# First scale of a decoder step by quarters, x first in the load queue, and inverse roots on turned columns

## The chip, the cores and the metric

The kernel runs on one core of one Trainium2 chip. The metric is the device time of one launch in microseconds. A core has five engines that run side by side and wait for each other through semaphores: TensorE (PE in the profile; PEld is its weight load) multiplies into PSUM, VectorE (DVE) and ScalarE (ACT) do elementwise work, GpSimd (POOL) does elementwise work on SBUF and issues some loads, and SyncE (SP) issues nearly all loads. The transfers themselves run on 16 DMA engines.

## The reference

One inference step of a one-layer recurrent decoder, in float32, for a prompt of 256 tokens and 8 sample sequences of 4 tokens, so for 288 token columns, with a model width of 2048. Nine condition vectors (one for the prompt, eight for the samples) give the adaLN shift, scale and gate. Cut to what matters here:

```python
mod = silu(c) @ w_ada + b_ada                      # c is (9, 2048), w_ada is (2048, 6*2048)
sh1, sc1, gt1, sh2, sc2, gt2 = split(mod, 6)
xn = rmsnorm(x, g_norm1) * (1.0 + sc1) + sh1       # rmsnorm: x * rsqrt(mean(x*x) + eps) * g
proj = xn @ w_in                                   # parts for a linear recurrence, GLA, mLSTM and gates
...                                                # three branches, each with its own norm and output product
x = x + gt1 * (merged @ w_out)
xn = rmsnorm(x, g_norm2) * (1.0 + sc2) + sh2
x = x + gt2 * (square(relu(xn @ w_ff1)) @ w_ff2)
y = rmsnorm(x, g_final)
```

The outputs are y and the new states of the three branches.

## The kernel before

Activations lie with features on the 128 partitions: x is 16 tiles (k = 0 to 15) of 128 features by 288 columns, eight tiles in each of the two slots xa and xb. Ten such slots of SBUF (s0 to s9) are used in turn for everything.

**Projections.** `stream` computes one block of 512 output features. A group is two k tiles of weights, 512 KB: `raw` is loaded on SP, ACT rounds it to `hi` (L156), DVE takes the rest `lo` = raw - hi (L157), and PE multiplies hi by the rounded activation xh, hi by its rest xl, and lo by xh (L163 to L165), so 4 x 2 x 3 = 24 matmuls of 288 columns a group. There are three buffers of each of raw, hi and lo. At the end of a block `evac` copies or adds the four PSUM banks to a slot: `to_slot` on ACT (L452), `plus_slot` on DVE (L463).

**Products with the conditions.** `cond_product` yields load units. A unit is a load of `w_ada` of 1 MB on SP into a slot, the ring tile or a pair of `st` tiles (the list `slots["ids"]` says which, in turn), and products of the nine conditions with it (L256): the output columns are dealt to four groups of 32 PE columns, so matmuls come in groups of four that run at once. After the last unit of a product `end` turns the result back with transposes of 32 by 32 blocks (L219), and `ada_finish` adds the bias (L278) and, for a scale, multiplies with g (L281). `units` lists all units in order: the scale of the first norm (SC1) in two halves of eight units each (`sc0`, `sc`), the shift (SH1) in 16, then a correction of the early projections for the shift (`cor`), and the rest.

**Order.** SP runs in the order of the program. On the other engines a planner orders the instructions by priority and by its own estimate of when they are ready, and each engine then runs its list in order. `every` gives a pattern with one word for each group of a stream: L loads the next unit, V (`visit`) multiplies all loaded units, right behind the last matmul so far; `drain` loads and multiplies until a product is done.

**The first stage.** x is loaded on ACT's queue while SP loads the eight units of `sc0`. ACT squares the 16 tiles, a product with ones sums them (L442), and `rstd_of` gives the inverse root as exp(-0.5 ln(..)) (L386, L387), each function with its own table load on ACT. Then `scale1(0)` makes xn without its shift for k = 0 to 7: `modulate` multiplies x by the root into a second tile (L395), scales the prompt columns on DVE (L400) and the sample columns on GpSimd (L402), and `split` makes xh (L424) and xl (L425). Three early blocks (NPRE, the features of q, k and half of v) run over k = 0 to 7, then, when `sc` is done, over k = 8 to 15 and are added. Meanwhile the units of the shift are multiplied, with the pattern

```python
every("L LV " * 4 + "L LLV L LV " * 3 + "LV" + " ." * 40)
```

`whole` rebuilds the scaled activation from xh and xl on GpSimd (L407), `shift` adds the shift (L414, L416) and splits again, and all further blocks use the result. The early blocks lack the shift's part, which `cor` adds later.

**Other inverse roots.** `rstd_of` serves the second norm (near 1172 us) and the final norm as well. `rows_rsqrt` serves the norms of the two branches (near 550 and 840 us): Sqrt on ACT over 288 columns and a reciprocal of 288 columns on DVE (L648). In `ev_o` a small activation with Ln (L1217) loads that table ahead of the second norm.

Of the kernel before, what the change touches and what calls it, by code (L numbers as in the profile page):

```python
# [14 lines left out]
P = 128  # L15
# [37 lines left out]
def trunk(ctx, tc, io):  # L53
# [149 lines left out]


    ct, th9 = (t288()[:, 0:KT * 9].rearrange("p (k c) -> p k c", k=KT) for _ in range(2))
# [35 lines left out]
    def cond_product(name, load, each, cols, stat, finish):  # L241
# [4 lines left out]
        def products(raw, q):  # L246
            if not acc_:
                acc_.append(pa.tile([P, 512], F32, tag="pa", name=nm("pa")))
# [26 lines left out]
    def ada_finish(kind):  # L275
        def finish(h, pv):
            o = mod[:, kind, 8 * h:8 * h + 8, :]
            V.tensor_tensor(out=o, in0=pv[:, :, 0:9], in1=bada[:, kind, 8 * h:8 * h + 8].unsqueeze(2).to_broadcast([P, 8, 9]), op=ALU.add)  # L278
            if kind in (SC1, SC2):
                gg = Pm("g1" if kind == SC1 else "g2")  # L280
                V.scalar_tensor_tensor(o, o, 1.0, gg[:, 8 * h:8 * h + 8].unsqueeze(2).to_broadcast([P, 8, 9]), ALU.add, ALU.mult)  # L281
        return finish
# [6 lines left out]
    def ada(kind):  # L289
# [92 lines left out]

    def rstd_of(ps):
        r = row("lf")
        with tc.high_priority():
            S.activation(r, ps[:, :N], AF.Ln, bias=eps, scale=1.0 / D)  # L386
            S.activation(r, r, AF.Exp, scale=-0.5)  # L387
        return r
# [4 lines left out]
    def modulate(xg, rs, k0, fk, xh, xl, xr):  # L393

        V.tensor_tensor(out=xr, in0=xg, in1=rs.unsqueeze(1).to_broadcast([P, 4, N]), op=ALU.mult)  # L395
        bc = [P, 2, NB, TS]
        for j in range(0, 4, 2):
            r = slice(k0 + j, k0 + j + 2)
            for i in range(j, j + 2):
                V.tensor_scalar(xr[:, i, 0:NP], xr[:, i, 0:NP], mod[:, fk, k0 + i, 0:1], None, ALU.mult)  # L400
            xs = smp(xr[:, j:j + 2])
            G.tensor_tensor(out=xs, in0=xs, in1=mod[:, fk, r, 1:9].unsqueeze(3).to_broadcast(bc), op=ALU.mult)  # L402
            split(xh[:, r, :], xl[:, r, :], xr[:, j:j + 2])

    def whole(k0, xh, xl, xr):

        G.tensor_tensor(out=xr, in0=xh[:, k0:k0 + 4, :].bitcast(F32), in1=xl[:, k0:k0 + 4, :].bitcast(F32), op=ALU.add)  # L407

    def shift(k0, shk, xh, xl, xr):

        for j in range(0, 4, 2):
            r = slice(k0 + j, k0 + j + 2)
            for i in range(j, j + 2):
                V.tensor_scalar(xr[:, i, 0:NP], xr[:, i, 0:NP], mod[:, shk, k0 + i, 0:1], None, ALU.add)  # L414
            xs = smp(xr[:, j:j + 2])
            V.tensor_tensor(out=xs, in0=xs, in1=mod[:, shk, r, 1:9].unsqueeze(3).to_broadcast([P, 2, NB, TS]), op=ALU.add)  # L416
            split(xh[:, r, :], xl[:, r, :], xr[:, j:j + 2])
# [9 lines left out]
    def halves(a, b):  # L427
        return lambda k: a[:, k, :] if k < 8 else b[:, k - 8, :]
# [984 lines left out]
```

## Time and profile before

| | |
|---|---|
| median of 3 runs | 2021.92 us (2020.87 to 2022.02) |
| profiled execution | 2018.23 us, of it 2016.5 us span |
| TensorE busy | 1962.6 us, 97% of the span |
| DVE, ACT, POOL busy | 1027.0, 805.7, 289.3 us |
| mean granted TensorE clock | 0.99 |
| DMA | 429.48 MB, mean 213 GB/s |

The profile shows one execution. Its page gives busy shares, the span in 40 slices, and the costliest groups of instructions by line, engine and operands. Other views answer questions about a stretch of time: the timeline lists instructions in order (start, duration, engine, line, operation, output <- input, count, and in brackets the idle time before with what ended it), the chain follows what released what, and the table by stage gives the busy time of each engine, the granted clock of TensorE, and the share and rate of the DMA engines. Instructions of a matmul on float32 that is not rounded stand twice in the records. Times of all views count from the start of the span.

### The profile page before, as it was taken

The page shows a single profiled execution, that of the slowest core. Times are in us where ns is not written, and L with a number is a line of the kernel's source. Part 1 is how long each engine was busy: PE and PEld are TensorE (multiplying, and loading weights), DVE is VectorE, ACT ScalarE, POOL GpSimd, SP SyncE. Part 2 cuts the span into 40 slices and gives each one's busy share as a digit, 9 for nine tenths or more (in the row PEclk, how much of TensorE's full clock was granted, in tenths as well). Part 3 has the DMA queues.
Part 4 walks back from the last instruction along what each step waited for, and adds up shares of the span by engine and source line. Part 5 has one row for each costly group of instructions (what it writes and reads, how often), then busy time and mean ns, then how long its engine had stood idle before and what let it go on. Part 6 is the DMA issues. An engine that isn't in the chain of part 4 may idle for free.

```text
span 2016.5 us, 35281 instructions
## 1 busy us (share of the span) xinstructions
PE 1962.6 (97%) x14838; PEld 1838.8 (91%) x14838; DVE 1027.0 (51%) x1436; ACT 805.7 (40%) x1107; POOL 289.3 (14%) x339
## 2 busy tenths in 40 slices
PE   6999999999999999899999999999999999999997
PEld 4889888999997998799999989999999999999997
DVE  3463647646692466543444564335444444444564
ACT  3333464533364332333333454443343434343434
POOL 0300200212231223100011441000010101010101
PEclk8999999999999999899999999999999999999998
DMA  9988756546642377676779736654444454455443
GB/s 372 397 325 308 269 199 237 205 168 240 211 153 73 124 259 253 209 258 250 263 257 356 272 123 224 230 197 159 174 160 157 163 182 158 159 173 171 157 159 119
DMA packets 119438, 429.48 MB, mean 213 GB/s; under 512 B 11744, under 2 KB 11904, under 8 KB 119152
## 3 DMA queue, kind: packets, MB, share of 16 engines
q1 hardware_dynamic: 109776, 392.56, 54.9%
q0 software_dynamic: 7920, 28.92, 4.0%
q10 hardware_dynamic: 1584, 5.75, 0.8%
q8 instruction: 116, 1.90, 0.4%
q14 instruction: 42, 0.34, 0.1%
HBM read 410.38 MB, written 16.81 MB: 212 GB/s over the span
## 4 chain that ended last, share of the span: by engine, by line
PE 87%; DMA 5%; DVE 4%; issue 2%; ACT 1%; POOL 0%; SPq 0%; DVEq 0%; ACTq 0%; POOLq 0%
PE mm L163 26%; PE mm L165 26%; PE mm L164 25%; PE pa L256 4%; DMA raw<-win 3%; DVE lo L157 1%; DMA st<-mC 1%; DVE s L530 1%; DMA s<-wada 1%; ACT hi L156 1%; DMA o_C_s<-st 0%; PE px L579 0%; PE px L1069 0%; PE pi L1113 0%; PE px L781 0%
## 5 line engine op out<-in xcount | busy, mean ns | idle before, releaser
L157 DVE TENSOR_TENSOR lo<-raw,hi 128x1024 fp32r<-128x1024 f32 x450 | 583.7, 1299 | 626.9 <-ACT hi L156 612.0
L156 ACT ACTIVATE hi<-raw 128x1024 fp32r<-128x1024 f32 x450 | 476.4, 1060 | 831.4 <-PE mm L164 618.2
L163 PE MATMUL mm<-xh,hi 128*128 128x288 f32 x2576 | 761.6, 299 | 11.8 <-ACT hi L156 4.7
L164 PE MATMUL mm<-xl,hi 128*128 128x288 f32 x2576 | 759.3, 297 | 0.1
L165 PE MATMUL mm<-xh,lo 128*128 128x288 f32 x2576 | 739.3, 297 | 4.4 <-DVE lo L157 4.4
L163 PEld LDWEIGHTS mm<-xh,hi 128*128 128x128 f32 x2576 | 484.6, 189 | 36.5 <-issue 17.8
L163 PE MATMUL mm<-s,hi 128*128 128x288 f32 x1664 | 489.4, 297 | 0.0
L164 PEld LDWEIGHTS mm<-xl,hi 128*128 128x128 f32 x2576 | 486.2, 189 | 3.4 <-issue 2.1
L164 PE MATMUL mm<-s,hi 128*128 128x288 f32 x1664 | 489.0, 296 | 0.0
L165 PEld LDWEIGHTS mm<-xh,lo 128*128 128x128 f32 x2576 | 478.7, 189 | 8.6 <-DVE lo L157 5.9
L165 PE MATMUL mm<-s,lo 128*128 128x288 f32 x1664 | 476.4, 295 | 0.4 <-DVE lo L157 0.4
L163 PEld LDWEIGHTS mm<-s,hi 128*128 128x128 f32 x1664 | 311.8, 188 | 6.1 <-issue 5.4
L164 PEld LDWEIGHTS mm<-s,hi 128*128 128x128 f32 x1664 | 312.5, 188 | 0.3
L165 PEld LDWEIGHTS mm<-s,lo 128*128 128x128 f32 x1664 | 308.2, 188 | 2.7 <-issue 1.7
L157 DVE TENSOR_TENSOR lo<-s,hi 128x1024 fp32r<-128x1024 f32 x80 | 98.0, 1225 | 115.3 <-ACT hi L156 115.3
L1251 POOL TENSOR_TENSOR t<-t 128x288 f32<-128x288 f32 x64 | 60.5, 954 | 647.6 <-ACT t L1250 647.6
L156 ACT ACTIVATE hi<-s 128x1024 fp32r<-128x1024 f32 x80 | 84.9, 1061 | 143.3 <-PE mm L164 140.0
L881 POOL TENSOR_TENSOR s<-s,t 128x288 f32<-128x288 f32 x32 | 32.2, 1030 | 207.3 <-DVE t L880 207.3
L1267 DVE TENSOR_TENSOR s<-s,mm 128x288 f32<-128x288 f32 x96 | 40.3, 451 | 33.9 <-PE mm L165 32.6
L256 PE MATMUL pa<-s,silc 128*32 128x512 f32 (+1 forms) x480 | 51.7, 526 | 5.5 <-DMA s<-wada 5.5
L425 DVE TENSOR_TENSOR s<-t,s 128x288 fp32r<-128x288 f32 x64 | 33.9, 568 | 16.6 <-ACT s L424 16.6
L1122 DVE SCALAR_TENSOR_TENSOR st<-st,csb,px 128x257 f32<-128x257 f32 x64 | 28.5, 479 | 23.6 <-PE px L1121 15.9
(358 smaller groups left out, 1144.7 us busy)
## 6 DMA issues: line engine op xcount, KB each, us to landing
raw<-win SPq DMA_DIRECT2D x192, 512.0 KB, 4.7
raw<-wf SPq DMA_DIRECT2D x176, 512.0 KB, 4.2
s<-wada SPq DMA_DIRECT2D x47, 1024.0 KB, 8.9
s<-wf SPq DMA_DIRECT2D x80, 512.0 KB, 3.5
ag<-wada SPq DMA_DIRECT2D x29, 1024.0 KB, 6.0
raw<-wout SPq DMA_DIRECT2D x32, 512.0 KB, 6.0
st<-wada SPq DMA_DIRECT2D x28, 512.0 KB, 6.8
s<-win SPq DMA_DIRECT2D x14, 768.0 KB, 6.8
```

What stands on the lines that cost most here:

```text
L156: pace["hi"] = S.activation(hi, raw, AF.Copy)
L157: pace["lo"] = V.tensor_tensor(out=lo, in0=raw, in1=hi.bitcast(F32), op=ALU.subtract)
L163: T.matmul(pss[m][:, :N], hi[:, kk, ms], xh, start=k == k0, stop=False)
L164: T.matmul(pss[m][:, :N], hi[:, kk, ms], xl, start=False, stop=False)
L165: pace["last"] = T.matmul(pss[m][:, :N], lo[:, kk, ms], xh, start=False, stop=k == kt - 1)
L256: pace["prod"] = T.matmul(ps[32 * j:32 * j + 32, h * w // 4:(h + 1) * w // 4], stat(k), v[:, j], start=k == 0 and h == 0, stop=k == KT - 1 ...
L425: V.tensor_tensor(out=dst_l[:, r], in0=src[:, r], in1=dst_h[:, r].bitcast(F32), op=ALU.subtract)
L530: V.scalar_tensor_tensor(y[:, m, s:NP], x[:, m, 0:NP - s], w[:, m, j:j + 1], y[:, m, s:NP], ALU.mult, ALU.add)
L881: G.tensor_tensor(out=a, in0=a, in1=t, op=ALU.add)
L1122: V.scalar_tensor_tensor(s4[:, i, d, :], s4[:, i, d, :], csb[:, h, b:b + 1], pu[:, 0:257], ALU.mult, ALU.add)
L1251: G.tensor_tensor(out=r, in0=r, in1=r, op=ALU.mult)
L1267: V.tensor_tensor(out=a, in0=a, in1=p, op=ALU.add)
```

## The change

- x is loaded on SP's queue, in four parts, behind the conditions and ahead of every unit of w_ada. Odd tiles are squared on DVE, even ones on ACT. A small Sqrt right after the first Tanh loads that table.
- x is multiplied by the inverse root in place, all 16 tiles, and later scaled and shifted in place; `whole` is gone, and the sample columns are scaled on DVE in place of GpSimd.
- SC1 comes in four quarters of four units each. A unit is four k tiles by 512 columns, so rows of 2 KB in place of 4 KB; its products have 128 columns in place of 256.
- The three early blocks run over k by quarters: for each quarter its scale, then three streams of two groups; the second to fourth quarter add with `plus_slot`. The units of the shift are loaded between those of the scale: two before the third quarter's, two before the fourth's, and the rest after. They are multiplied into the PSUM bank of `longp`, beside the scale's. A written list gives the slots, a new pattern the visits.
- `inv_sqrt` replaces exp(-0.5 ln(..)) and the long root and reciprocal: it turns the 288 columns, which are equal over the partitions of a block, with 32 by 32 transposes, takes 9 columns through Sqrt and the reciprocal, and turns them back.

The diff, cut to its core:

```diff
+    xa, xb = slot(0), slot(1)
+    xin = halves(xa, xb)
+    for i in range(4):
+        Q.dma_start((xa, xb)[i // 2][:, 4 * (i % 2):4 * (i % 2) + 4, :], io["x"][:, 4 * i:4 * i + 4, :])
     S.activation(th9, ct, AF.Tanh, scale=0.5)
+    S.activation(sc([P, 1], "warm", 1), th9[:, 0, 0:1], AF.Sqrt, bias=eps, scale=0.0)
...
-        return cond_product(kind, load, 1, 2048, silu_c, ada_finish(kind))
-
-    def ada_half(name, kind, h):
+        return cond_product(kind, load, 1, 2048, silu_c, ada_finish(kind), longp if kind == SH1 else None)
+
+    def ada_quarter(kind, i):
 
         def load(raw, q):
-            Q.dma_start(raw[0].rearrange("p (k m) -> p k m", k=2), wada[kind, h, 2 * q:2 * q + 2].rearrange("k p m -> p k m"))
-        return cond_product(name, load, 2, 1024, silu_c, lambda _, pv: ada_finish(kind)(h, pv))
+            Q.dma_start(raw[0].rearrange("p (k m) -> p k m", k=4),
+                        wada[kind, i // 2, 4 * q:4 * q + 4, :, 512 * (i % 2):512 * (i % 2) + 512].rearrange("k p m -> p k m"))
+        return cond_product(f"sc{i}", load, 4, 512, silu_c, ada_finish(kind, 4 * i))
...
     def units():
-        yield from ada_half("sc0", SC1, 0)
-        yield from ada_half("sc", SC1, 1)
-        yield from ada(SH1)
+        sh1 = ada(SH1)
+        yield from ada_quarter(SC1, 0)
+        yield from ada_quarter(SC1, 1)
+        for i in (2, 3):
+            yield next(sh1)
+            yield next(sh1)
+            yield from ada_quarter(SC1, i)
+        yield from sh1
...
+    def inv_sqrt(r, src, **ka):
+
+        with tc.high_priority():
+            t = t288()
+            V.transpose(t, src)
+            c = sc([P, N // 32], "rsc", 1)
+            S.activation(c, t[:, 0:N:32], AF.Sqrt, **ka)
+            V.reciprocal(c, c)
+
+            V.transpose(r.rearrange("p (a b) -> p a b", b=32), c.unsqueeze(2).to_broadcast([P, N // 32, 32]))
+        return r
+
     def rstd_of(ps):
-        r = row("lf")
-        with tc.high_priority():
-            S.activation(r, ps[:, :N], AF.Ln, bias=eps, scale=1.0 / D)
-            S.activation(r, r, AF.Exp, scale=-0.5)
-        return r
+        return inv_sqrt(row("lf"), ps[:, :N], bias=eps, scale=1.0 / D)
...
+    def modulate(k0, op, kind, step=2):
+
+        x = (xa, xb)[k0 // 8][:, k0 % 8:k0 % 8 + 4, :]
+        for j in range(0, 4, step):
+            r = slice(k0 + j, k0 + j + step)
+            for i in range(j, j + step):
+                V.tensor_scalar(x[:, i, 0:NP], x[:, i, 0:NP], mod[:, kind, k0 + i, 0:1], None, op)
+            xs = smp(x[:, j:j + step])
+            V.tensor_tensor(out=xs, in0=xs, in1=mod[:, kind, r, 1:9].unsqueeze(3).to_broadcast([P, step, NB, TS]), op=op)
+            split(xh[:, r, :], xl[:, r, :], x[:, j:j + step])
...
     for k in range(KT):
         sq = t288()
-        S.activation(sq, xin(k), AF.Square)
+        if k % 2:
+            V.tensor_tensor(out=sq, in0=xin(k), in1=xin(k), op=ALU.mult)
+        else:
+            S.activation(sq, xin(k), AF.Square)
         T.matmul(ps[:, :N], ones, sq, start=k == 0, stop=k == KT - 1)
     rs = rstd_of(ps)
+    for k in range(0, KT, 4):
+        t = (xa, xb)[k // 8][:, k % 8:k % 8 + 4, :]
+        V.tensor_tensor(out=t, in0=t, in1=rs.unsqueeze(1).to_broadcast([P, 4, N]), op=ALU.mult)
...
-    every("L LV " * 4 + "L LLV L LV " * 3 + "LV" + " ." * 40)
-    for b in range(NPRE):
-        run(stream(win, B_Q + b, act1, 8, to_slot((qk, vv)[b // 2], 4 * (b % 2))))
-    drain("sc")
-    scale1(1)
-    for b in range(NPRE):
-        run(stream(win, B_Q + b, act1, KT, plus_slot((qk, vv)[b // 2], 4 * (b % 2)), k0=8))
-    xrs = [(xs3, xs4)[i % 2][:, 4 * (i // 2):4 * (i // 2) + 4, :] for i in range(4)]
-    for i in range(4):
-        whole(4 * i, xh, xl, xrs[i])
+    slots.update(ids=(2, 5, 6, 7, None, "st", 3, 4, 2, 5, 6, 7, 3, 4, 2, 5, None, "st", 6, 7, 3, 4, 2, 5, None, "st", 6, 7), n=0)
+    every("LL LL . V LL LL" + " L L V LL L L" * 3)
+    for q in range(4):
+        drain(f"sc{q}")
+        with tc.high_priority():
+            modulate(4 * q, ALU.mult, SC1, 1 if q == 0 else 2)
+        if q == 0:
+            G.tensor_copy(con[:, 0:1], mod[:, SC1, 0, 0:1])
+            G.dma_start(con, io["con"])
+        for b in range(NPRE):
+            to = plus_slot if q else to_slot
+            run(stream(win, B_Q + b, act1, 4 * q + 4, to((qk, vv)[b // 2], 4 * (b % 2)), k0=4 * q))
     drain(SH1)
     with tc.high_priority():
-        for i in range(4):
-            shift(4 * i, SH1, xh, xl, xrs[i])
+        for q in range(4):
+            modulate(4 * q, ALU.add, SH1)
...
         if add is None:
-            S.activation(r, p[:, :N], AF.Sqrt, bias=eps, scale=1.0 / 256)
-        else:
-            V.scalar_tensor_tensor(r, p[:, :N], 1.0 / 256, add, ALU.mult, ALU.add)
-            S.activation(r, r, AF.Sqrt)
-        V.reciprocal(r, r)
-        return r
+            return inv_sqrt(r, p[:, :N], bias=eps, scale=1.0 / 256)
+        V.scalar_tensor_tensor(r, p[:, :N], 1.0 / 256, add, ALU.mult, ALU.add)
+        return inv_sqrt(r, r)
...
             if k == KT - 4:
-                S.activation(sc([P, 1], "warm", 1), ssum[:, 0:1], AF.Ln)
+                S.activation(sc([P, 1], "warm", 1), ssum[:, 0:1], AF.Sqrt)
```

More of the change, by code (lines that the diff above doesn't have):

```diff
@@ L239, in raw_tile, with cond_product @@
         return [flat(slot(i))[:, 0:2048]]
-    def cond_product(name, load, each, cols, stat, finish):
+    def cond_product(name, load, each, cols, stat, finish, bank=None):
         acc_ = []
@@ L273, in cond_product, with ada_finish @@
             yield name, ld, lambda raw, q=q: products(raw, q), end if q == n - 1 else None
[L275 removed]
+    def ada_finish(kind, k0=0):
         def finish(h, pv):
[L277 to L278 removed]
+            n = pv.shape[1]
+            r = slice(k0 + 8 * h, k0 + 8 * h + n)
+            o = mod[:, kind, r, :]
+            V.tensor_tensor(out=o, in0=pv[:, :, 0:9], in1=bada[:, kind, r].unsqueeze(2).to_broadcast([P, n, 9]), op=ALU.add)
             if kind in (SC1, SC2):
                 gg = Pm("g1" if kind == SC1 else "g2")
[L281 removed]
+                V.scalar_tensor_tensor(o, o, 1.0, gg[:, r].unsqueeze(2).to_broadcast([P, n, 9]), ALU.add, ALU.mult)
         return finish
@@ L405, in whole @@
[L405 to L417, printed above, removed]
+    def modulate(k0, op, kind, step=2):
[7 more added lines that the diff above has]
+            split(xh[:, r, :], xl[:, r, :], x[:, j:j + step])
@@ L453, in to_slot @@
         return f
[L456 removed]
+    slots.update(ids=(8, 9, 3, 4), n=0)
     drain("sc0")
[L458 removed]
     qk, vv = slot(8), slot(9)
```

32 lines of the change are left out of this document (3 added, 29 removed).

## The prediction

> **What bounds the kernel now.** First the page's busy shares and the forty slices:
>
> ```profile
> PE 1962.6 (97%) x14838; PEld 1838.8 (91%) x14838; DVE 1027.0 (51%) x1436; ACT 805.7 (40%) x1107; POOL 289.3 (14%) x339
> PE   6999999999999999899999999999999999999997
> ```
>
> TensorE (PE) is full in all slices but the first and the last, so a change gains only what it takes out of PE's gaps or work. The diff touches the first slice, the stage up to about 145 us and four inverse roots. So next the timeline of the start, the end of that stage, and the table by stage:
>
> ```profile
> 32.98 1.06 ACT L156 ACTIVATE hi<-raw 128x1024 fp32r<-128x1024 f32 x1 [12.34 <-DMA raw<-win]
> 38.11 1.33 PE L163 MATMUL mm<-xh,hi 128*128 128x288 f32 x4 [4.54 <-ACT xh L424]
> 132.21 0.78 DVE L219 STREAM_TRANSPOSE t<-pa 128x256 f32<-128x256 f32 x2 [3.10 <-PE pa L256]
> 144.06 0.37 PE L163 MATMUL mm<-xh,hi 128*128 128x288 f32 x1 [2.18 <-DVE s L463]
> core 0: us, PE busy (x) PEld busy (x) DVE busy (x) ACT busy (x) POOL busy (x), PEclk, DMA share, GB/s
> 0.00:33.00 33.00, 21.59 (x156) 10.81 (x160) 3.53 (x9) 10.91 (x23) 1.44 (x8) 0.85 0.91 353
> 38.00:44.00 6.00, 5.83 (x24) 5.49 (x25) 6.00 (x8) 3.20 (x5) 0.25 (x1) 0.54 1.03 408
> 50.00:80.00 30.00, 30.00 (x278) 26.72 (x276) 11.34 (x19) 11.34 (x18) 2.07 (x4) 1.00 1.01 398
> 141.00:145.00 4.00, 1.82 (x14) 1.61 (x13) 4.00 (x12) 1.98 (x3) 0.00 (x0) 1.00 1.03 401
> ```
>
> The first projection matmul starts at 38.1. From there PE hardly stops until 141.9 (144.06 less its idle 2.18): the early projections (3 blocks in 8 groups of 24 matmuls) and the products of scale and shift. Meanwhile DMA is full too (share 1.01). So PE and the load queue are both near their limits here, and an earlier start is worth only what the queue allows.
>
> **The change, part by part.** *Start.* Sizes from the list of loads, and durations from the chain:
>
> ```profile
> s<-x ACTq DMA_DIRECT2D x4, 576.0 KB, 8.8
> s<-wada SPq DMA_DIRECT2D x28, 1024.0 KB, 9.4
> raw<-win SPq DMA_DIRECT2D x57, 512.0 KB, 6.5
> con<-con POOLq DMA_DIRECT2D x1, 313.0 KB, 6.7
> 44.24 0.53 PE mm L163 x4
> 47.45 1.86 PE pa L256 x32
> 49.31 0.33 PE mm L163
> 81.22 2.71 PE pa L256 x24
> ```
>
> Before, raw weights 0 land at 32.98, behind x (2.36 MB) and eight scale loads (8.39 MB). After, x and four loads stand ahead of them; 4.2 MB less at 400 GB/s is 10.5 us, so they land near 22.5, and the first matmul comes at about 24.5: the last sc0 product, its transpose and finish, one scaled tile. But the order is then two loads, raw 1, two loads, raw 2: raw 2 has behind it all that raw 0 has now, plus two raws and con, 1.37 MB or 3.4 us. It lands at 36.4, its rounding (1.06) ends at 37.5. So the third group starts only 0.6 us before today's first. What is gained is two groups done by then: 24 x 0.1325 = 3.2 us each, 6.4, and the half-clock stretch that today lies on the path (clock 0.54 in 38 to 44: 24 matmuls in 5.8 us, 2.6 too many). Sum 0.6 + 6.4 + 2.6 = **9.6 us**. The first matmul could slip to 28.5 (37.5 less 6.4 and 2.6) without cost; only past that does the first scale not come early enough, which would be the change not doing what it says. That slack hides the sixteen squares (half of them now on DVE, about an L463 each) and their root, x times rs (four L395, below, 5.4 us on DVE) and the four x issues on SP, and it is why the earlier start as such is not worth 14 us.
>
> *Products.* A visit of two half-scale units (eight groups of four at 256 columns) is 1.86, one of three shift units (six groups at 512, so twelve such lengths) 2.71: 0.2125 a group and 0.16 fixed, with 0.2 more in the slow matmul behind it (0.33). A unit of either kind is 0.85, a visit's own cost 0.36. A quarter unit has eight groups at 128 columns instead of four at 256: half the streaming, 0.106 a group, but the same four weight loads:
>
> ```profile
> 90.85 0.13 PEld L256 LDWEIGHTS pa<-s,silc 128*32 128x32 f32 x4 [0.30 <-issue]
> ```
>
> So between 0.85 (loads hidden) and 1.04 (0.13 a group); I take 0.95, midway, as the row does not say how much of a load overlaps. On the path before: 8 scale and 16 shift units in 11 visits, 20.4 + 4.0 = 24.4 us. After: 12 and 16 in 5 visits, 11.4 + 13.6 + 1.8 = 26.8. **Loss 2.4 us** (1.2 to 3.5).
>
> *The end of the stage.* Rows by shape for the stage:
>
> ```profile
> L157 DVE TENSOR_TENSOR lo<-raw,hi 128x1024 fp32r<-128x1024 f32 x58 | 73.9, 1280 | 86.8 <-ACT hi L156 84.6 <-PE pa L256 2.2
> L425 DVE TENSOR_TENSOR xl<-s,xh 128x576 fp32r<-128x576 f32 x16 | 11.5, 755 | 0.0
> L424 ACT ACTIVATE xh<-s 128x576 fp32r<-128x576 f32 x16 | 10.1, 676 | 10.6 <-DVE s L400 6.4 <-DVE s L416 4.2
> L463 DVE TENSOR_TENSOR s<-s,mm 128x288 f32<-128x288 f32 x12 | 5.4, 455 | 7.8 <-PE mm L165 7.4
> L395 DVE TENSOR_TENSOR s<-s,row 128x1152 f32<-128x1152 f32 x4 | 5.2, 1354 | 11.9 <-ACT row L387 11.9
> L414 DVE TENSOR_SCALAR s<-s,mod 128x256 f32<-128x256 f32 x16 | 5.0, 352 | 0.0
> L416 DVE TENSOR_TENSOR s<-s,mod 128x64 f32<-128x64 f32 x8 | 1.8, 224 | 0.0
> 134.02 0.37 DVE L278 TENSOR_TENSOR mod<-t,par 128x72 f32<-128x72 f32 x2
> 2005.91 0.44 ACT L387 ACTIVATE row<-row 128x288 f32<-128x288 f32 x1
> 2006.39 1.73 DVE L1295 TENSOR_TENSOR s<-s,row 128x576 f32<-128x576 f32 x2 [4.34 <-ACT row L387]
> ```
>
> Today the last shift product ends at 132.1 and its chain hides under ten us of early projections. After, six shift units are multiplied behind the last projection, and everything after them is bare: transposes 0.78, finish 0.37, two L414 0.7, L416 0.2, xh 0.68, seven hops of 0.04 (2006.35 to 2006.39 in the last two rows): 3.0 us, with one lo (1.28) in between 4.3, plus 0.5 until xl is there: 4.8, against today's 2.2. **Loss 2.6 us** (0.8 to 4.5).
>
> *Cover inside the stage.* The visits of the next quarter's products stand two or three groups (6.4 or 9.6 us) ahead of its first matmul, more than that chain, so the three inner boundaries cost nothing; uncovered, each costs up to 4.8. DVE has per quarter six lo (7.7), twelve adds L463 (5.5; 24 more adds in all, which also read PSUM), scaling and xl (3.4), in 24 us of PE: 70%. Behind a transpose that waits for products, the lo's and adds stand in DVE's order. The sums that GpSimd did (whole) vanish off the path; its scaling of the samples costs DVE eight L416, inside the 70%. SP waits for slots 3 and 4 at the visit of the third quarter with two units and two raws issued ahead, about 8 us of queue: nothing lost.
>
> *Clock.* Before the third group PE waits about 3.4 us. A gap of 4.5 us preceded today's half-clock stretch. If the clock falls again, the third group runs at half for 2.8 to 6.8 us, a loss of 1.4 to 3.4; if not, nothing. I take **1.4**. The Trainium skill (TensorE: Matmul & The Clock Gate, "What's actually happening") has free windows of about 3.4 us, one idle one halving the clock; by it the gap lies on the edge, and the loss, an estimate, is 0 or 1.7.
>
> Early stage: 9.6 - 2.4 - 2.6 - 1.4 = **3.2 us** gained.
>
> *Inverse roots.* Last one, on the path to the end:
>
> ```profile
> 2001.32 2.42 PE L381 MATMUL pi<-t,ones 128*128 128x288 f32 x8 [0.24 <-ACT t L375]
> 2002.81 1.28 ACT L386 ACT_TABLE_LOAD   x1
> L1217 ACT ACTIVATE warm<-row x1: 203/203/203, 1146.2 to 1146.2; 128x1 f32<-128x1 f32 x1
> L548 DVE RECIPROCAL lam<-lam 128x8 f32<-128x8 f32 x1 | 0.2, 200 | 0.0
> ```
>
> The sums end at 2003.74; today the root takes until 2006.39 (row above), 2.65 us, a second table load in it. After: a transpose of 288 columns (0.39 for 256, from the two at 132.21; taken as 0.5), root 0.2, reciprocal 0.2, transpose 0.5, five hops of 0.04: 1.6. **Gain 1.0** (0.7 to 1.3); a load for Sqrt would still hide under the sums. In the middle (about 1172) the root gains at most as much, but PE is filled with held products until 1174.0:
>
> ```profile
> 1172.11 1.90 PE L256 MATMUL pa<-s,silc 128*32 128x512 f32 x16
> 1174.40 0.80 PE mm L163 x4
> 845.99 1.06 ACT L156 ACTIVATE hi<-raw 128x1024 fp32r<-128x1024 f32 x1 [5.70 <-DMA raw<-win]
> ```
>
> so 0.3 remains. The root near 840 loses a long reciprocal, but the matmuls behind it wait for raw weights that round at 846: nothing. Sqrt in place of Exp at the start leaves one more table load (1.28) for the first Tanh or Exp of the recurrent branch, on ACT: 0 to 1.3, taken as nothing since PE is full there.
>
> Sum 3.2 + 1.0 + 0.3 = **4.5 us** off the profiled execution's 2018.23 (span 2016.5 and 1.7 around it): 2013.7. The median of the runs lies 3.7 higher, 2021.92, so 2017.4.
>
> **Rivals.** *The queue is slower with half rows.* Quarter loads have rows of 2 KB instead of 4. Against it, 160 to 168 us, where most packets are 2 KB rows of the shift correction, beside 50 to 80:
>
> ```profile
> DMA packets 1344, 3.19 MB, mean 398 GB/s; under 512 B 74, under 2 KB 74, under 8 KB 1343
> DMA packets 3145, 11.94 MB, mean 398 GB/s; under 512 B 238, under 2 KB 238, under 8 KB 3141
> ```
>
> Up to the last shift load the queue carries x, 32 units, 24 raws and con, 48.8 MB, and about 0.4 of small constants (11.65 MB by 33 less the 11.27 named). At 398 these 49.2 MB have landed by 33 + 37.6 / 0.398 = 127.3, seven us ahead of PE. Were it 353 throughout, as in the first 33 us: 139.4, and 6 us of product and chain give 145.4: 1.3 lost, 1.3 gained at the roots, 2021.9. The Trainium skill (DMA: Bandwidth & Descriptors, "Where 436 GB/s comes from") says that for loads from HBM the HBM side, about 358 GB/s, binds; the trace's 398 over 30 us disagrees. By that figure, as an estimate, the time would be 2019.9. Chance 0.06, no change.
>
> *Faster: the last shift products slip ahead of the last projections.* They are bound to no place, and their data are there. Then the chain is hidden as today, and no clock is lost; with products at their low end 9.6 - 1.2 = 8.4, and 1.3: 2012.2. The queue's limit (127.3 + 1.2 + 4.3 = 132.8) would give 11.3 and 1.3, 2009.3. For it: data lie ready; against: PE's order follows the program where nothing waits. Chance 0.17.
>
> *Slower: the quarter boundaries become gaps.* Three inner boundaries, each with DVE's order between visit and first matmul. It decides when that chain (4.3 with one lo in it) passes the 6.4 or 9.6 us of cover: five adds (2.3) or two more lo's ahead of it do at the first. Each then loses about 1 us of waiting and a half-clock stretch of 6.8 us (3.4): 3 x 4.4 = 13.2 if all three, 2030.6; the likelier two, 8.8 - 4.5 = 4.3 lost, 2026.2. For it: DVE 70% full, in order. Against: DVE is 100% busy in 141 to 145 only. Chance 0.19.
>
> **How the numbers follow.** About 0.2% (4 us) can be told from no change. Forecast 0.58: its terms' ends reach from 0 to 8 gained, and 4.5 lies just beyond the bound: 0.37 faster, 0.20 same, 0.01 slower. Fast rival 0.17 faster; slow queue 0.06 same; gaps 0.18 slower, 0.01 same. Together 0.54, 0.27, 0.19. Range: the forecast's own is 2014 to 2022; down to 2010 takes in most of the fast rival, up to 2025 the boundary gaps in one place.
>
> **What would show it.** Right: first projection matmul at 23 to 26; a PE gap of 2 to 4 us before the third group, near 37; quarter visits of four units near 4.1 us; PE through with the early projections and shift products at 134 to 138; first matmul of the next block at 139 to 143; last root within 1.7 us of the sums. Wrong: DMA under 370 GB/s in 40 to 120; PE idle over 1 us before a second, third or fourth quarter; the first stage ending before 136 or after 146; any later stage whose length differs by more than 2 us.

## The result and the profile after

The changed kernel takes 2157.57 us (median of 4 runs, 2155.66 to 2158.7), against 2021.97 us of the kernel before: ratio 1.0665, interval 1.0647 to 1.0684. It is 135.6 us slower where 4.5 us faster was forecast, and far outside the range. The profiled execution took 2157.55 us, its span 2155.8.

The page after, busy share of TensorE, its forty slices, and the clock granted in them:

```profile
PE 2020.2 (94%) x15118; PEld 1875.8 (87%) x15118; DVE 1028.5 (48%) x1499; ACT 797.9 (37%) x1096; POOL 268.1 (12%) x327
PE   7989999986999746999999999999999999999997
PEclk9999999985999855999999999999999999999999
```

The line of slices that was full before now has two holes, at slices 9 and 10 and at 14 to 16 (54 us each), and the clock falls in both. They lie far behind the stage that the prediction was about. To place the loss, compare when the n-th projection matmul (L163 to L165, 12,720 in each kernel) starts in the two traces. The lag is after minus before, in us, each from one profiled execution. Two executions of one kernel (f4 and g3 below, e4 and g4 likewise) differ in it by under 1 us at the 624th matmul and by up to 4 us at the 4600th, so only differences above that count:

| n-th projection matmul | starts before at | lag after |
|---|---|---|
| 0 | 38.11 | -10.67 |
| 48 | 49.24 | -10.12 |
| 336 | 101.65 | -8.24 |
| 480 | 127.73 | -8.25 |
| 577 (second of the next block) | 144.27 | +6.60 |
| 624 | 150.48 | +11.00 |
| 2300 | 444.24 | +11.31 |
| 3400 | 623.32 | +69.91 |
| 4600 | 873.97 | +141.21 |
| 7000 | 1230.94 | +139.91 |
| 12719 | 2000.79 | +139.91 |

Three steps: the 10 us gained at the start become 11 lost by the end of the first stage; 58.6 go between the 2300th and the 3400th matmul; 71.3 more by the 4600th. Behind that the lag changes little: it falls by 0.7 near 970 us, and by about 0.6 at the root of each of the two full norms (139.3 at the end of the span).

*The two holes.* The table by stage of the kernel after, inside them (columns: window, its length, busy time and count of PE, PEld, DVE, ACT, POOL, then granted clock, DMA share, GB/s), and a stretch of the kernel before in the same loop:

```profile
core 0: us, PE busy (x) PEld busy (x) DVE busy (x) ACT busy (x) POOL busy (x), PEclk, DMA share, GB/s
460.00:520.00 60.00, 35.75 (x154) 17.82 (x152) 20.61 (x53) 8.04 (x18) 22.44 (x20) 0.58 0.35 123
742.00:850.00 108.00, 54.20 (x216) 26.12 (x216) 31.32 (x78) 5.73 (x11) 23.13 (x32) 0.50 0.46 147
```

```profile
440.00:500.00 60.00, 59.61 (x462) 54.92 (x461) 39.01 (x52) 21.85 (x32) 16.55 (x13) 1.00 0.62 218
```

PE is busy 60% and 50% of the time, at a mean clock of 0.58 and 0.50, and no other engine is busy more than 40%: 154 matmuls in 60 us where there were 462. The timeline of PE, SP and DVE there, and then the waits (waiting engine and line, releaser, us in total, times, longest; the last line is of the whole span):

```profile
480.19 1.08 PE L813 MATMUL pi<-st,s 128*32 128x256 f32 x8 [6.90 <-DMA st<-gla]
495.57 1.08 PE L813 MATMUL pi<-st,s 128*32 128x256 f32 x8 [7.29 <-DMA st<-gla]
...
431.41 5.07 SPq L155 DMA_DIRECT2D raw<-win  x2
518.86 0.48 DVE L403 STREAM_TRANSPOSE t<-pi 128x288 f32<-128x288 f32 x1 [2.94 <-PE pi L639]
519.27 0.74 DVE L227 STREAM_TRANSPOSE t<-pa 128x256 f32<-128x256 f32 x2
522.06 0.38 SPq L305 DMA_DIRECT2D ag<-wada  x1
...
849.14 0.48 DVE L403 STREAM_TRANSPOSE t<-row 128x288 f32<-128x288 f32 x1
849.55 1.51 DVE L875 SCALAR_TENSOR_TENSOR t<-ag,mm 128x288 f32<-128x288 f32 x4
```

```profile
SPq L305 <- PE pa L264: 85.5, 1, 85.5
...
PE pi L1108 <- DMA st<-mC: 46.8, 13, 7.6
...
SPq L155 <- DVE lo L157: 1340.3, 365, 163.0
```

In the loops over the states of the two branches (gla at L813, mC at L1108) PE has nothing but the branch's own products, and the state products wait up to 7.6 us for a load. Before, projection matmuls stood between them. Why they no longer do shows, for the first loop, on SP's line: its queue issues nothing from 436 to 522 us. It stands once for 85.5 us at the load of a condition unit into the ring tile (ag, L305), which waits for a product's visit (pa, L264), and all later raw weights are queued behind it on SP. The product before it (pa) had its last matmul at 418, but its result is turned back (L227) only at 519.27, right behind the first transpose of the branch's root (L403, 518.86). The second loop is cut off in another way: there SP stands 163.0 us at a raw weight, for a buffer that lo (L157) has yet to read. PE runs no projection matmul between 694.9 and 850.6 us, and the DVE operations that empty the PSUM banks of the output product (ev, L875) come at 849.55, again right behind the first transpose of a root (849.14).

The order of the instructions as they are built says the same. Projection matmuls that stand on PE between the first and the last state product of each loop:

| kernel | first loop (gla) | second loop (mC) |
|---|---|---|
| before | 529 | 887 |
| after | 0 | 0 |

*The first stage.* Start, second stop, and the end of the stage in the timeline after:

```profile
27.44 1.33 PE L163 MATMUL mm<-xh,hi 128*128 128x288 f32 x4 [5.19 <-ACT xh L433]
39.12 0.40 PE L163 MATMUL mm<-xh,hi 128*128 128x288 f32 x1 [2.70 <-ACT hi L156]
...
60.19 0.34 SPq L155 DMA_DIRECT2D raw<-win  x1
71.07 0.37 SPq L311 DMA_DIRECT2D s<-wada  x1
79.85 0.53 PE L163 MATMUL mm<-xh,hi 128*128 128x288 f32 x2 [2.04 <-ACT hi L156]
...
129.25 0.90 SPq L155 DMA_DIRECT2D raw<-win  x1
141.86 0.37 SPq L318 DMA_DIRECT2D s<-win  x1
145.30 0.78 DVE L227 STREAM_TRANSPOSE t<-pi 128x256 f32<-128x256 f32 x2 [1.42 <-PE pi L264]
148.78 1.06 ACT L156 ACTIVATE hi<-raw 128x1024 fp32r<-128x1024 f32 x1 [6.16 <-DMA raw<-win]
149.74 2.39 ACT L433 ACTIVATE xh<-s 128x576 fp32r<-128x576 f32 x4
150.47 1.33 PE L163 MATMUL mm<-xh,hi 128*128 128x288 f32 x4 [5.22 <-ACT xh L433]
```

SP stops from 60.2 to 71.1 and again from 130.2 to 141.9, each time at a load whose slot is not free. The first stop makes raw weights late and PE idle at 77.8. The second holds back the raw weights for the next block; ACT, which runs in order, waits for them 6.16 us (until 148.78) with xh of the new activation queued behind. DMA is therefore no longer full (table by stage), and the waits of SP for slots in 20 to 147 us add up to over 48 us (second fence):

```profile
50.00:80.00 30.00, 27.36 (x339) 25.13 (x328) 15.06 (x34) 9.14 (x13) 0.00 (x0) 1.00 0.87 328
125.00:145.00 20.00, 20.00 (x172) 12.76 (x164) 7.31 (x11) 3.17 (x3) 0.00 (x0) 1.00 0.79 284
```

```profile
SPq L311 <- PE pa L264: 18.1, 3, 10.5
SPq L305 <- PE pi L264: 17.3, 2, 9.3
SPq L318 <- PE pi L264: 13.2, 2, 11.6
```

*The last root*, chain of the kernel after:

```profile
2141.24 2.43 PE pi L397 x8
...
2143.77 0.49 DVE t L403
...
2144.88 0.49 DVE row L408
...
2145.39 0.76 DVE s L1290
```

From the end of the sums (2143.67) to the scaling (2145.39) it takes 1.72 us, against 2.65, with no table load in it.

### The profile page after: what moved, and what is told of

The parts are those of the page before. It is cut to its first block, busy times and chain, and to the rows that moved or that the text cites. A ratio compares the mean times of both kernels' runs of the same rounds, so it can differ in the third digit from the quotient of the medians.

```text
span 2155.8 us, 35896 instructions
## 1 busy us (share of the span) xinstructions
PE 2020.2 (94%) x15118; PEld 1875.8 (87%) x15118; DVE 1028.5 (48%) x1499; ACT 797.9 (37%) x1096; POOL 268.1 (12%) x327
## 4 chain that ended last, share of the span: by engine, by line
PE 86%; DMA 6%; DVE 3%; issue 2%; ACT 1%; SPq 1%; POOL 1%; DVEq 0%; POOLq 0%; ACTq 0%
PE mm L163 26%; PE mm L165 25%; PE mm L164 25%; PE pa L264 4%; DMA raw<-win 2%; DMA st<-mC 2%; DMA o_C_s<-st 1%; PE pi L264 1%; DMA st<-gla 1%; DVE lo L157 1%; SPq L311 1%; PE px L1116 1%; ACT hi L156 0%; POOL s L674 0%; SPq L155 0%
## 5 line engine op out<-in xcount | busy, mean ns | idle before, releaser
L157 DVE TENSOR_TENSOR lo<-raw,hi 128x1024 fp32r<-128x1024 f32 x450 | 562.4, 1251 | 693.0 <-ACT hi L156 677.3
L163 PE MATMUL mm<-xh,hi 128*128 128x288 f32 x2576 | 763.8, 300 | 21.5 <-ACT xh L433 10.4
L165 PE MATMUL mm<-xh,lo 128*128 128x288 f32 x2576 | 743.5, 298 | 6.0 <-DVE lo L157 6.0
L163 PEld LDWEIGHTS mm<-xh,hi 128*128 128x128 f32 x2576 | 487.5, 190 | 39.8 <-ACT hi L156 13.0
L163 PE MATMUL mm<-s,hi 128*128 128x288 f32 x1664 | 490.2, 297 | 1.8 <-ACT s L861 1.8
L165 PEld LDWEIGHTS mm<-xh,lo 128*128 128x128 f32 x2576 | 483.1, 190 | 8.7 <-DVE lo L157 8.2
L165 PE MATMUL mm<-s,lo 128*128 128x288 f32 x1664 | 475.7, 295 | 0.4 <-DVE lo L157 0.4
L163 PEld LDWEIGHTS mm<-s,hi 128*128 128x128 f32 x1664 | 312.0, 188 | 9.4 <-issue 5.9
L165 PEld LDWEIGHTS mm<-s,lo 128*128 128x128 f32 x1664 | 307.9, 188 | 1.9 <-issue 0.8
L157 DVE TENSOR_TENSOR lo<-s,hi 128x1024 fp32r<-128x1024 f32 x80 | 98.0, 1225 | 114.9 <-ACT hi L156 114.9
L1246 POOL TENSOR_TENSOR t<-t 128x288 f32<-128x288 f32 x64 | 60.2, 951 | 645.0 <-ACT t L1245 645.0
L1108 PE MATMUL pi<-st,s 128*32 128x257 f32 x128 | 16.5, 605 | 46.9 <-DMA st<-mC 46.8
L1108 PEld LDWEIGHTS pi<-st,s 128*32 128x32 f32 x128 | 3.1, 136 | 51.7 <-DMA st<-mC 51.3
```

The source lines that it names most:

```text
L157: pace["lo"] = V.tensor_tensor(out=lo, in0=raw, in1=hi.bitcast(F32), op=ALU.subtract)
L163: T.matmul(pss[m][:, :N], hi[:, kk, ms], xh, start=k == k0, stop=False)
L165: pace["last"] = T.matmul(pss[m][:, :N], lo[:, kk, ms], xh, start=False, stop=k == kt - 1)
L1246: G.tensor_tensor(out=r, in0=r, in1=r, op=ALU.mult)
```

## The experiments

**The hole: theories.** T: the tile that the new root takes. `inv_sqrt` takes one tile of the ring `t288` (five tiles, dealt out in the order of the program), and in `rows_rsqrt` it is held until a branch's root is done; a later user of the same place in the ring has to wait for that. H: the high priority of the root draws the whole branch ahead of the projections. E: the new order of the first stage upsets what comes later.

*e1_own_tile*: the changed kernel, the branch roots in the tile of a row (`lf`) that is idle there.

```diff
-    def inv_sqrt(r, src, **ka):
+    def inv_sqrt(r, src, t=None, **ka):
-            t = t288()
+            t = t288() if t is None else t
...
-            return inv_sqrt(r, p[:, :N], bias=eps, scale=1.0 / 256)
+            return inv_sqrt(r, p[:, :N], row("lf"), bias=eps, scale=1.0 / 256)
...
-        return inv_sqrt(r, r)
+        return inv_sqrt(r, r, row("lf"))
```

> The changed kernel, but the roots of the two branches turn their columns into the tile r_lf (idle there) and not into one of the five t288 tiles. Theory T (ring): the new t288 tile, taken in the middle of a branch, makes all later users of that ring wait for the branch's end, so the state loops ran without projections between them; without it the 128 us between the 2300th and the 4600th projection matmul go, and the time is 2157.5 - 128 = 2029 +- 4, 11 us of it lost up to the 600th matmul. Rival E (early stage): the other order of the first stage upsets the planner later on; then nothing changes, 2157. Rival H (high priority of the new roots): nothing changes, 2157.

Measured: 2032.59 us (7 runs), ratio 1.0054 (1.0038 to 1.007). 125 us are gone with one tile. The clock line of its page has one slice below 9, the first:

```profile
PEclk8999999999999999999999999999999999999999
```

*e2_ring_only*: the kernel before, its old root, and only a tile of the ring taken in `rows_rsqrt`, with two copies of one column.

```diff
         V.reciprocal(r, r)
+        t = t288()
+        V.tensor_copy(t[:, 0:1], r[:, 0:1])
+        V.tensor_copy(r[:, 0:1], t[:, 0:1])
```

> The kernel before with its own roots, and behind the two branch roots one t288 tile that one column is copied into and back. Theory T: this one tile alone costs the same 128 us, 2018 + 128 = 2146 +- 8, with no projection matmul inside the two state loops. Rivals E and H: two copies of one column, no time, 2018 to 2020.

Measured: 2147.74 us (one run), 127 us more than the kernel before (2020.91), and the same two holes:

```profile
PEclk8999999976999756999999999999999999999999
```

No root was changed here, nor anything in the first stage: one ring tile per branch is enough. E falls for this part of the loss.

*e3_no_priority*: the changed kernel, the branch roots at normal priority, ring tile kept.

```diff
-        with tc.high_priority():
+        with tc.high_priority() if ahead else nullcontext():
...
-            return inv_sqrt(r, p[:, :N], bias=eps, scale=1.0 / 256)
+            return inv_sqrt(r, p[:, :N], ahead=False, bias=eps, scale=1.0 / 256)
...
-        return inv_sqrt(r, r)
+        return inv_sqrt(r, r, ahead=False)
```

> The changed kernel with the branch roots at normal priority; t288 still in them. Theory T: nothing changes, 2157 +- 4. Rival H: the loops get their projections back, 2029. Rival E: 2157, so this run tells T from H only.

Measured: 2151.27 us (one run), 2 us below the range that T expected and far from the 2029 us of H. H falls.

*e4_roots_only*: the kernel before with all four roots on turned columns, the branches' in the row `lf`; the first stage as before.

> The kernel before with all four roots on turned columns, the branch ones by way of r_lf; first stage as before. Theory T: no loss, and the roots bring what the lag between the traces shows, 0.6 at the last norm, 0.6 in the middle, and up to 1 near 840: 2016.5 +- 1.5 against 2018.2, a ratio of 0.9992. Rival H: the priority unsettles the loops, 2140 or more. Rival E: about as before, 2017 to 2019.

Measured: 2017.74 us (12 runs), ratio 0.9983 (0.997 to 0.9997); measured again (*g4_roots_again*) 2017.84, 0.9984 (0.9972 to 0.9996). So the roots alone are worth about 3 us, and what is left of the loss, 11 us or more, is the first stage.

**Who passes the wait on.** Theory L: in each branch it is one user of the ring that passes the root's wait on. Two users of the ring were given a tile of their own, one at a time, with the roots still on the ring. *g1_turn_tile*: `by_feature`, which turns back the result of a product with the conditions.

```diff
-        t = t288()[:, 0:n]
+        t = sp.tile([P, N], F32, tag="bf", name=nm("bf"), bufs=1)[:, 0:n]
```

> The changed kernel, with the roots still on the ring of five tiles; only the tile into which the result of a product with the conditions is turned back (by_feature) comes from a place of its own. Theory L: in the first branch the root's ring tile passes its wait on to exactly this user of the ring. Then the 529 projection matmuls stand among the state products of the first loop again, and the second loop keeps none: of the 128 us the 58.6 lost between the 2300th and the 3400th projection matmul come back, 2099 us (2090 to 2105), ratio 1.034 to 1.041. The lag behind the kernel before is about +11 at the 3400th and +80 at the 4600th. Rival M: the wait is passed on by several users of the ring at once, or by the root itself, and one tile changes nothing: 2157 us, ratio 1.0665, lag +70 at the 3400th.

*g2_output_tile*: the same edit to `t` in `ev` of the output products (L874).

> The changed kernel, with only the tile that the branches' output products go through (ev, second branch) in a place of its own. Theory L: in the second branch it is this user of the ring that passes the wait on. Then the first loop stays empty and the second has projection matmuls among its state products again: the 70 us lost behind the 3400th matmul come back, 2087 us (2080 to 2095), ratio 1.029 to 1.036, lag +70 at the 3400th matmul and about +75 at the 4600th. Rival M: nothing changes: 2157 us, ratio 1.0665, lag +140 at the 4600th.

Measured: g1 2104.24 us (4 runs), ratio 1.0407 (1.0385 to 1.0428); g2 2100.13 us (4 runs), 1.0384 (1.0359 to 1.041). The clock lines of the two pages:

```profile
PEclk9999999999999558999999999999999999999999
```

```profile
PEclk8999999995999999969999999999999999999999
```

g1 has lost the first hole alone, g2 the second, but for a smaller dip at slice 18 (0.6). In g1 PE runs the first loop like the kernel before, while the second stays half empty:

```profile
450.00:520.00 70.00, 69.60 (x539) 63.27 (x538) 44.90 (x59) 24.65 (x36) 21.23 (x16) 1.00 0.61 219
680.00:790.00 110.00, 56.08 (x229) 27.19 (x220) 34.26 (x84) 3.85 (x11) 30.46 (x34) 0.55 0.42 139
```

The orders as built and the lags against the kernel before agree:

| kernel | first loop | second loop | lag at 3400 | lag at 4600 |
|---|---|---|---|---|
| after | 0 | 0 | +69.91 | +141.21 |
| e1, roots off the ring | 529 | 887 | +17.02 | +18.98 |
| e2, before and one ring tile | 0 | 0 | +60.46 | +129.63 |
| e3, no priority | 0 | 0 | +66.69 | +135.05 |
| g1, by_feature off the ring | 529 | 0 | +13.54 | +88.59 |
| g2, ev off the ring | 0 | 584 | +67.83 | +78.87 |

Theory L holds for both loops. g1 came out inside its range; g2 missed its own by 5 us: 57 of 70 came back. 584 of 887 matmuls stand in the second loop again; what holds up the rest was not tried. So the path is shown at its ends in the first branch: the root holds a tile, the transposes of a condition product need that place of the ring, the product's visit is late, SP stands at the next condition load, and the raw weights stand behind it. In the second branch the tile that the output product is written to (t in ev) passes on most of it. The links between (the visit, the PSUM banks, SP) are read from the times and waits above, and no run took them away singly.

**The first stage.** On the base of e1. Theory Q: SP's stops at occupied slots cost the stage, through late raw weights and idle PE; visits at other groups and slots in another order remove them. Rival C: the chain and the lost clock at the end of the stage cost the same whatever the slots do. The first three have one run each. Kernels whose first stage is that of e1 (after, e3, g2) stand at +10.3 to +11.0 at the 624th matmul.

*f1_cor_slots*: the first loads of the correction go into the slots that come free first.

```diff
-    slots.update(ids=(5, 6, 7, None, 0, 1, 3, 4), n=0)
+    slots.update(ids=(3, 4, 5, 6, 7, None, 0, 1), n=0)
```

> As e1, but the first loads of the correction go to slots 3 and 4, which are free at that time, and not to slot 5, whose unit is multiplied last. Theory Q (the load queue stood): raw weights behind that load come early, ACT's rounding no longer holds up xh, the first matmul of the next block comes 2 to 3 us sooner than 150.7 (147.5 to 148.5), the half-clock stretch behind it gets shorter, and the lag at the 624th projection matmul falls from +10.3 to +2 to +8. Rival C (the chain from product to xh sets it): first matmul within 1 us of 150.7, lag +9 to +11.

Measured: 2027.98 us; lag at the 624th matmul +9.83, against +10.27 in e1. The timeline at the end of the stage:

```profile
147.20 1.33 PE L163 MATMUL mm<-xh,hi 128*128 128x288 f32 x4 [2.85 <-ACT xh L433]
151.95 0.61 PE L164 MATMUL mm<-xl,hi 128*128 128x288 f32 x1 [3.41 <-DVE xl L434]
```

The first matmul is 3.1 us earlier than in e1 (150.31) and the idle time before it 2.85 in place of 5.46, as Q has it, but the next wait (xl, behind other work on DVE) is 3.41 in place of 0.80, and the clock is 0.66 in 145 to 160 in both: on the whole nothing is won here, as C has it.

*f2_more_visits*: one visit more, in the first group of the second to fourth quarter.

```diff
-    every("LL LL . V LL LL" + " L L V LL L L" * 3)
+    every("LL LL . V LL LL" + " LV L V LL L L" * 3)
```

> As e1, with one visit more at the start of the second to fourth quarter, so that the slots of the next loads are free sooner. Theory Q: SP's wait from 60 to 71 us shrinks, the gap of 2.0 us near 78 and the half-clock stretch behind it go, and the lag at the 528th projection matmul falls from -1.6 to -4 to -6. Rival D (DVE order: lo that comes late): the gap stays within 0.5 us, and the 0.4 us of each visit come on top: lag -1.5 to 0.

Measured: 2024.65 us; lag -5.68 at the 528th matmul (e1 -1.59) and +4.65 at the 624th (e1 +10.27). The gap near 78 and the half clock behind it are gone, as Q has it. At the end of the stage two waits stay:

```profile
143.09 0.79 PE L163 MATMUL mm<-xh,hi 128*128 128x288 f32 x4 [2.55 <-ACT xh L433]
147.48 0.61 PE L164 MATMUL mm<-xl,hi 128*128 128x288 f32 x1 [3.60 <-DVE xl L434]
```

*f3_kept_warm*: 20 matmuls of no use are put behind the last product of the shift, so that PE is busy while the chain runs.

```diff
     drain(SH1)
+    with tc.high_priority(), tc.issue_after(pace["prod"].ins):
+        p = misc()
+        for i in range(20):
+            T.matmul(p[:, :N], ones, rs, start=i == 0, stop=i == 19)
```

> As e1, with 20 products of ones and the root's tile behind the last shift product, 4.8 us on PE in the gap of 5.2; their result is read by nobody. Theory K (clock): the granted clock stays at 1.0 from 148 to 159, the first matmul of the next block comes at 150.5 to 151.5 as before, and the lag at the 624th projection matmul falls from +10.3 to +6 to +7. Without that theory: +10 to +11.

Measured: 2032.5 us. The timeline and the table by stage:

```profile
145.93 9.97 PE L489 MATMUL px<-row,ones 128*128 128x288 f32 x40
```

```profile
145.00:160.00 15.00, 15.00 (x83) 12.06 (x77) 13.95 (x38) 7.67 (x11) 0.00 (x0) 1.00 0.98 349
```

They took 9.97 us, not 4.8 (matmuls on unrounded float32 stand twice, 40 records of 0.25), so they delayed the next block themselves. But the clock stays at 1.00, where it is 0.70 in 145 to 162 of the kernel after, and the lag is flat, +11.60 at the 577th and +11.64 at the 624th, where e1 goes from +6.45 to +10.27. The lag at the 624th missed the +6 to +7 expected, because of the late start. Of the 3.8 us by which e1 loses more behind the start of the block, 0.80 is its wait for xl, which here had 5 us longer to come; about 3 us are left for the half clock.

*f4_all_early*: both at once, thought through for the whole stage: more visits, a slot order that follows them, and two groups of projections left behind the last visit of the shift.

```diff
-    slots.update(ids=(2, 5, 6, 7, None, "st", 3, 4, 2, 5, 6, 7, 3, 4, 2, 5, None, "st", 6, 7, 3, 4, 2, 5, None, "st", 6, 7), n=0)
-    every("LL LL . V LL LL" + " L L V LL L L" * 3)
+    slots.update(ids=(2, 5, 6, 7, None, "st", 3, 4, 2, 5, 6, 7, None, 3, 4, 2, "st", 5, 6, 7, None, 3, 4, 2, "st", 5, 6, 7), n=0)
+    every("LL LL . V LL LL" + " L LV L LL L ." + " L LV L LL LV L" + " LL LV LL LLV . .")
...
-    slots.update(ids=(5, 6, 7, None, 0, 1, 3, 4), n=0)
+    slots.update(ids=(3, 4, None, 5, 6, 7, 0, 1), n=0)
```

> As e1, with visits every two or three groups, slots dealt in the order in which they come free, all shift units loaded and multiplied two groups ahead of the end of the early projections, and the correction's first loads in free slots. By theory Q the chain of the shift is then covered again: early projections done at 136 to 140 against 141.6 before, next block at 138 to 142 against 144.3, lag at the 624th matmul -2 to -6; with the roots' 3 us the whole is 5 to 9 us under the kernel before, ratio 0.9955 to 0.9975. Rival D: lag 0 to +6, ratio 0.998 to 1.002.

Measured: 2017.02 us (12 runs), ratio 0.9977 (0.9965 to 0.9989), just above the 0.9955 to 0.9975 expected; lag at the 624th matmul -3.49, as expected. The table by stage, the waits of SP for slots, and the end of the stage:

```profile
23.00:80.00 57.00, 49.58 (x578) 46.67 (x568) 28.89 (x57) 22.10 (x33) 0.73 (x2) 0.91 1.02 388
80.00:120.00 40.00, 39.91 (x420) 34.22 (x422) 23.13 (x40) 9.91 (x11) 0.00 (x0) 1.00 1.00 395
120.00:160.00 40.00, 38.67 (x300) 33.57 (x288) 26.67 (x54) 15.56 (x19) 0.00 (x0) 1.00 0.85 307
```

```profile
SPq L305 <- PE pi L264: 8.5, 2, 8.1
SPq L311 <- PE pa L264: 7.0, 2, 6.2
SPq L311 <- PE pi L264: 5.8, 1, 5.8
```

```profile
129.14 2.76 PE L264 MATMUL pi<-s,silc 128*32 128x512 f32 x24
131.83 0.40 PE L163 MATMUL mm<-xh,hi 128*128 128x288 f32 x1
```

DMA is full to 120 us, SP's waits for slots have halved, the matmuls go on at 131.83 behind the last visit without a gap, and there is no half clock behind 80 us. So the order of visits and slots was worth 14 us of the stage (+10.27 in e1, -3.49 here). How much of that is Q's is not settled, since f4 also leaves two groups behind the last visit and so covers the chain of C. The lag tells where it was won. At the 528th matmul f4 is 2 us ahead of e1 (-3.53 and -1.59) and has all shift products done, of which 4.5 us are still to come in the kernel after (140.75 to 145.25 us). From there to the 624th the lag stays as it is, where e1 loses 11.9 us and f2 10.3.

*g3_all_early_again* ran beside the roots alone, to part the two gains.

> The same kernel as in f4_all_early, beside g4_roots_again, to tell how much of its gain is the start's and how much the roots'. Theory Q: the start is 3.5 us ahead at the 624th projection matmul, and the rest of the two kernels is alike, so it ends 3 to 4 us before the other: ratio 0.9965 to 0.998 here, 0.998 to 0.9993 there. Rival V: what the start gains is lost again to the order of the later parts, and the two agree within 1 us.

> The same kernel as in e4_roots_only: the first stage of before, all four roots on turned columns, the branches' in a tile of their own. Theory Q: ratio 0.998 to 0.9993, 3 to 4 us behind g3_all_early_again. Rival V: within 1 us of it.

Measured: 2013.30 us (12 runs), ratio 0.9961 (0.9947 to 0.9975), beside 2017.84 (12 runs) of the roots alone, 0.9984 (0.9972 to 0.9996). The first ratio is a little under the 0.9965 to 0.998 expected, the second inside its range. The start is 4.0 us ahead at the 624th matmul (-4.16 and -0.19), and the medians are 4.5 apart; the two intervals touch. In the earlier runs (f4 and e4) the two stood 0.0006 apart in ratio, here 0.0023; the 4.0 us of the traces are 0.0020. So this version beats the kernel before by 5 to 8 us (2022.07 and 2021.03 beside it), and that the early start adds to the roots is likely but not settled by the times alone.

## Why the prediction was wrong

- **The step that failed first** is "the root near 840 ... : nothing", and with it that the root near 550 was not costed at all. They were priced as arithmetic (a shorter reciprocal that nobody waits for), and so they are (e4). The added instruction that mattered was the one that takes a tile: `t = t288()` in a branch whose root ends late. It cost 58.6 and 71.3 us, 130 of the 139 by which the profiled execution is longer. No rival had it; "any later stage whose length differs by more than 2 us" was named as what would show it wrong, and did.
- **The first stage** was forecast to gain 3.2 us and lost 11.0, so 14.2 are to be explained. The third group came at 39.12, not 37.5 (1.6). PE waited 2.3 us for hi and 1.8 for lo (0.6 three times) in 43 to 146, where nothing was forecast, and lost 1.7 more at half clock behind the wait near 78. The boundary chain took 5.2 in place of 4.8. What comes behind it was not forecast at all: 4.4 between the 577th and the 624th matmul, most of it half clock (3.8 in e1 against f3). Together 12.2, with 0.3 more of clock near 40 us (1.7 for 1.4) 12.5; 1.7 us stays unexplained. About 1.0 of the 4.4 is a wait for xl at 152.8.
- Two steps stand behind that. One is "SP waits for slots 3 and 4 ... about 8 us of queue: nothing lost". SP stood 10.5 and 11.6 us at a time. The 8 us of loads already issued were less than that, and the raw weights are behind it in the same queue. f2 shows it for the first stop: with that wait (L311) at most 5.9 us, against 10.2 in e1, the lag is 4.1 us better at the 528th matmul.
- The other is "Loss 2.6 us" for the **end of the stage**. It had its chain nearly right (5.2 for 4.8) but took the chain for the only cost. In f1 the next wait takes back what the first gives, and the half clock behind it stays. The fast rival's mechanism, the chain under the last projections, is what f4 does by its pattern, and there the stage gains 3.5 to 4.2 us.
- **Right were the parts worked out from rows.** The start: the first matmul came at 27.44, 3 us later than the 24.5 worked out and outside the 23 to 26 named, but inside the slack to 28.5, and the gap before the third group was 2.70 us (2 to 4). The products: 26.3 us (26.8); a visit of four quarter units 3.70 (4.1 forecast). The last root: 1.72 us (1.6), gain 0.9 (1.0) in its chain, though 0.6 at the end of the span. The middle root: the lag falls by 0.6 across it (0.3). The roots together, 1.3 us, were set low: e4 gives about 3 (ratios 0.9983 and 0.9984), though 1.3 is inside the interval.
- **The rivals.** The slow queue is refuted. Its sign came, DMA at 355 GB/s in 40 to 120 us (under 370), with 328 in 50 to 80; but it fell because SP stood: with the same loads in another order f4 moves 388 and 395 in 23 to 120 us. That settles the Trainium skill's rule (DMA: Bandwidth & Descriptors, "Where 436 GB/s comes from") for this stage too: its HBM limit of about 358 GB/s does not hold here. The boundary rival was wrong too: no later quarter began behind an idle time; the wait of 2.04 us near 78 lies inside the second quarter and is for raw weights.
- **The clock** fell behind the 2.70 us before the third group (0.72 in 38 to 44 us) and cost 1.7 us. The window of about 3.4 us that the Trainium skill gives (TensorE: Matmul & The Clock Gate, "What's actually happening") had left both cases open; here an idle time shorter than that window was enough. That it fell in this execution was partly luck: in f1 the gap at the same place was 3.52 us, and the clock stayed at 1.00 in 38 to 44 us.

## What to carry to other kernels

A tile of a rotating pool is a resource like an engine: before an edit takes one inside a branch that ends late, ask which users come next in the ring, in the order of the program, and whether something that feeds the main loop is among them. The count of filler instructions between the first and the last of a loop's own, in the order as built, matched what the times showed: the loops that had none in the kernel after, g1 and g2 lost 57 to 75 us. It can be taken before a run. A load queue that stands at an occupied slot stops everything behind it, so the points where products free slots have to follow the order of the loads.

## What the runs showed of the hardware that was not expected

- A half-empty TensorE ran at half clock most of that time: 0.58 on the mean in 60 us at 60% busy and 0.50 in 108 us at 50% busy. Whether the clock fell because of the waiting or of something else was not tried apart; where the matmuls came back (g1, first loop) it was 1.00.
- The length of an idle time alone does not tell whether the clock falls. In the kernel after, 2.04 us at 77.8 was followed by a clock of 0.66 in 79 to 84; in the kernel before, 2.18 us in front of 144.06 was followed by 1.00 up to 149, and in f1 3.52 us in front of 39.52 by 1.00. Of the three waits of 0.6 us none was followed by a fall. In front of the block at 150 the idle time of 5.2 us was followed by half clock up to 158.9, about 4 us lost; with filler matmuls (f3) the clock stayed at 1.00.
- Rows of 2 KB did not slow the load queue: f4 moved 388 GB/s in 23 to 80 us, when half of the bytes came in such rows, and 395 in 80 to 120, when over nine tenths came in rows of 4 KB, against 398 in 50 to 80 us of the kernel before with rows of 4 KB.
